# A hybrid encoder layer: where dense projections run beside the DeltaNet inverse, where the normalised operand is made, and how inverses and attention rows are finished

## The chip, the cores and the metric

The kernel runs on one core of one Trainium2 chip. The metric is device time in microseconds, the median of several runs of the whole program. One further execution was taken with the hardware profiler, and every row below is from it. The core's engines are TensorE (PE, with its weight loads as PEld), VectorE (DVE), ScalarE (ACT), GpSimd (POOL) and SyncE (SP, which here only issues DMAs). Each works through a queue of its own in order; semaphores tie them together.

## The reference, cut to what matters

There are two layers of width 1024 over 512 tokens, all float32.

```
h    = rms_norm(x, norm_mix)                    # x * rsqrt(mean(x*x)) * g
proj = h @ w_in                                 # q k v | dqkv z alpha beta | rwkv
y_att = window attention(q, k, v, sink)         # 6 heads, rotary, softmax over +-128 tokens
y_dn  = gated DeltaNet(conv(dqkv), z, ...)      # 6 heads, two directions, chunks of 64
y_rw  = RWKV-7(rwkv, ...)                       # 4 heads, two directions, chunks of 64
x = x + concat(y_att, y_dn, y_rw) @ w_out
x = x + conv_ffn(rms_norm(x, norm_ffn))
```

The DeltaNet and RWKV parts each need, for every chunk of 64 tokens, head and direction, the inverse of a unit triangular 64x64 matrix. Then a scan walks through the eight chunks. After the second layer a last rms_norm follows.

## The kernel before, in words

Activations lie transposed: 128 channels on the partitions, 512 tokens along the free axis. A float32 product is made of three fp32r products: both operands are split into a high and a low part, and `product` adds high x high, high x low and low x high in PSUM. A projection of 128 output columns has 8 blocks of 128 rows, so 24 matmuls of 512 columns (L332 to L334). The weights come by DMA in pieces of four blocks into one of three `wr` buffers; ScalarE makes the high part (L321) and GpSimd subtracts it to get the low part (L322), each with three buffers. The norm's factor `rb` (one number for each token) isn't applied before the projection: `Norm.tile_done` splits x times g, and each user of a projection multiplies its result by `rb` on VectorE while it moves it out of PSUM (`token_shift` L474, `dn_conv` L685, `rope` L867, `gate_proj` L975 and so on).

A layer goes through these steps in program order. Eight projections give RWKV's inputs. `rwkv_prep` runs for two head pairs, with DeltaNet projections and their 5-tap convolutions (`dn_conv`, four taps on VectorE, L691 and L693) between. The RWKV inverse is a chain of 30 steps of two VectorE operations on 32x32 blocks (`invert`, L403 and L404). `finish_inverse` completes the 64x64 inverses from 32x32 blocks by small matmuls (L455, L461) and copies on ScalarE (L457, L465, L469). `rwkv_scan` walks through eight steps; `dn_prep` for the three DeltaNet pairs and the five attention projections are written between them. Then `rwkv_out` runs, and the DeltaNet inverse for both directions at once (`invert_both`, L432 and L433), with an attention step after every sixth of its 31 turns. An attention step (`attn_head`) is one block of 128 queries of a pair of heads: scores (L886), masked and with a row maximum (L887), exponentials on ScalarE (L896), rows scaled by 1/sum on VectorE (L900), transposes (L903, copied by L905) and the product with v (L907). There are twelve such steps. `finish_inverse` for DeltaNet follows, then three gate projections (`gate_proj`), `dn_scan` with the remaining attention steps, `dn_out`, and the output projection: for each of eight column blocks 24 matmuls over attention, RWKV and DeltaNet rows, added to the residual (L1068). The feed-forward block ends the layer.

The queues are not simply in program order. The program is written in Tile, which at build time puts the instructions of each engine in an order: of those that are ready it takes the one that program order asks for first. An allocation waits for a free buffer of its tag. PSUM has 8 banks: two for stream `j` (dense products), three for `r`, two for `d`, one for `o`. The tag `p4` has 20 tiles of 4 KB a partition, which hold nearly everything of a layer that lives long; `t2` tiles are the short-lived 2 KB ones.

Of the kernel before, what the change touches and what calls it, by code (L numbers as in the profile page):

```python
# [14 lines left out]
P = 128  # L15
T = 512
# [20 lines left out]
def _const_array():  # L37
# [23 lines left out]
    add("m32", np.stack([hi32 - 1.0, -hi32], 1))  # L61
# [54 lines left out]
def trunk(tc, t, out):  # L116
# [21 lines left out]
    def p4(*free, dt=F32):  # L138
        return bp.tile([P, *free], dt, tag="p4", bufs=20, name=nm("p4"))
# [94 lines left out]


# [26 lines left out]
    def split(src, gcol, tag, k):  # L262
        hi = bp.tile([P, T], F32R, tag=f"hh{k}", bufs=1, name=nm("hh"))
        lo = bp.tile([P, T], F32R, tag=f"hl{k}", bufs=1, name=nm("hl"))
# [71 lines left out]
    def proj(l, parts, c0, m=P, heads=None):  # L336
# [7 lines left out]
        o = ps("j")  # L344
# [100 lines left out]
    def finish_inverse(st, o1, o2, units, upper, sign):  # L445

        ra, rb = (0, 32) if upper else (32, 0)
        n = len(units)
        for g0 in range(0, n, 16):
            grp = units[g0 : g0 + 16]  # L450
            py = ps(st)
# [7 lines left out]
            for i, (p, mt, c) in enumerate(grp):  # L459
                for h in (0, 64):  # L460
                    PE.matmul(pw[h + ra : h + ra + 32, 32 * i : 32 * i + 32], yt[h + rb : h + rb + 32, i, :], o1[h + rb : h + rb + 32, p, :], start=True, stop=True)  # L461
            for i in range(0, len(grp), 8):
                mt = grp[i][1]
# [219 lines left out]
    def dn_conv(l, o, i, rb, dst):  # L683
        u = t2("d")
        V.tensor_tensor(u, o, rb, mult)  # L685
# [466 lines left out]
```

## Time and profile before

| what | value |
|---|---|
| median of three runs | 1710.0 us (1709.49, 1710.0, 1717.93) |
| profiled execution, its own time | 1722.8 us |
| its span, first to last instruction | 1721.0 us |
| mean granted TensorE clock | 0.931 |
| TensorE busy | 1544.2 us, 90% |
| VectorE busy | 973.5 us, 57% |
| ScalarE busy | 792.0 us, 46% |
| GpSimd busy | 638.7 us, 37% |

Busy time is the time in which at least one instruction of an engine is recorded as running; matmuls overlap each other, so the mean duration of one is longer than its share of a full TensorE. [...] Times inside the profile count from the start of the span. The second layer's mixers run from about 866 to 1350 us, its feed-forward block after that.

### The profile page before, as it was taken

What the parts mean: (1) busy time and instruction counts of PE and PEld (TensorE: products, weight loads), DVE (VectorE), ACT (ScalarE), POOL (GpSimd) and SP (SyncE); (2) the same over time, 40 slices, a digit from 0 to 9 for tenths busy, and PEclk for the clock granted to TensorE, in tenths of its full rate; (3) what the DMA queues carried; (4) which work ended last, traced back from release to release, by engine and by line L of the source; (5) the groups of instructions that cost most, each with busy time, mean ns of one, the idle gap of its engine ahead of it and who ended that gap; (6) DMA issues with size and microseconds to landing.
All of it is one profiled execution on the core that took longest, in us unless ns stands there. A gap on an engine that the chain in (4) does not pass through costs nothing. (4 is left out here: it accounts for less than half of the span.)

```text
span 1721.0 us, 29049 instructions
## 1 busy us (share of the span) xinstructions
PE 1544.2 (90%) x11500; PEld 1208.7 (70%) x11500; DVE 973.5 (57%) x1595; ACT 792.0 (46%) x1493; POOL 638.7 (37%) x510
## 2 busy tenths in 40 slices
PE   7988889569999999999998887983899999999997
PEld 4676666347778888888876666652677788888885
DVE  6578946875535557731136797579563555555001
ACT  5547453355444444433336654351734544444321
POOL 4321323101265554445552112420104555555553
PEclk9989979669999999999999998995799999999998
DMA  6221211100143333333442012220003333333331
GB/s 185 73 57 38 56 38 44 37 2 20 36 122 96 98 98 95 96 104 114 119 101 68 25 45 50 55 70 1 4 19 93 102 95 97 98 99 114 101 101 65
DMA packets 230536, 126.07 MB, mean 73 GB/s; under 512 B 23656, under 2 KB 221416, under 8 KB 230400
## 3 DMA queue, kind: packets, MB, share of 16 engines
q1 hardware_dynamic: 228624, 121.02, 25.0%
q10 hardware_dynamic: 1776, 3.20, 0.6%
q8 instruction: 90, 1.47, 0.3%
q14 instruction: 46, 0.38, 0.1%
HBM read 117.84 MB, written 6.34 MB: 72 GB/s over the span
## 5 line engine op out<-in xcount | busy, mean ns | idle before, releaser
L322 POOL TENSOR_TENSOR wl<-wr,wh 128x512 fp32r<-128x512 f32 (+1 forms) x408 | 553.6, 1363 | 753.2 <-ACT wh L321 664.2
L332 PE MATMUL ps<-hh,wh 128*128 128x512 f32 x1248 | 505.2, 405 | 22.1 <-ACT wh L321 19.6
L333 PE MATMUL ps<-hl,wh 128*128 128x512 f32 x1248 | 504.5, 404 | 0.0
L334 PE MATMUL ps<-hh,wl 128*128 128x512 f32 x1248 | 500.9, 401 | 0.4 <-POOL wl L322 0.4
L321 ACT ACTIVATE wh<-wr 128x512 fp32r<-128x512 f32 (+1 forms) x408 | 246.2, 615 | 330.8 <-PE ps L333 262.4
L332 PEld LDWEIGHTS ps<-hh,wh 128*128 128x128 f32 x1248 | 237.8, 191 | 80.9 <-ACT wh L321 20.4
L333 PEld LDWEIGHTS ps<-hl,wh 128*128 128x128 f32 x1248 | 238.0, 191 | 56.8 <-issue 4.2
L334 PEld LDWEIGHTS ps<-hh,wl 128*128 128x128 f32 x1248 | 237.5, 190 | 56.8 <-issue 3.9
L1104 DVE TENSOR_TENSOR p<-ps,p 128x512 f32<-128x512 f32 x16 | 11.1, 692 | 196.6 <-PE ps L334 196.6
L332 PE MATMUL ps<-p,wh 128*128 128x512 f32 x256 | 99.6, 389 | 0.0
L333 PE MATMUL ps<-p,wh 128*128 128x512 f32 x256 | 99.6, 389 | 0.0
L334 PE MATMUL ps<-p,wl 128*128 128x512 f32 x256 | 99.6, 389 | 0.0
L903 PE MATMUL ps<-fixed,cv 128*128 128x128 f32 x120 | 24.9, 340 | 62.4 <-DVE cv L900 62.0
L1081 DVE TENSOR_TENSOR tr<-ps,rb 128x512 f32<-128x512 f32 x44 | 30.4, 691 | 80.9 <-PE ps L334 80.8
L292 POOL TENSOR_TENSOR tr<-tr,tr 128x512 f32<-128x512 f32 x32 | 42.6, 1332 | 70.4 <-ACT tr L285 59.9
L903 PEld LDWEIGHTS ps<-fixed,cv 128*128 128x128 f32 x120 | 16.0, 168 | 72.5 <-issue 44.8
L1084 DVE SCALAR_TENSOR_TENSOR td<-tr,fixed,td 128x511 f32<-128x511 f32 x44 | 42.8, 972 | 37.7 <-ACT td L1083 37.7
L285 ACT ACTIVATE tr<-p 128x512 f32<-128x512 f32 x36 | 22.6, 628 | 85.9 <-DVE p L1104 64.4
L791 POOL TENSOR_TENSOR sm<-sm,fixed 128x384 f32<-128x384 f32 x12 | 10.8, 896 | 121.5 <-DVE sm L820 64.5
L333 PEld LDWEIGHTS ps<-p,wh 128*128 128x128 f32 x256 | 48.1, 188 | 10.1
L332 PEld LDWEIGHTS ps<-p,wh 128*128 128x128 f32 x256 | 48.1, 188 | 10.1
L1084 DVE SCALAR_TENSOR_TENSOR tr<-td,fixed,tr 128x511 f32<-128x511 f32 x44 | 33.9, 771 | 37.5 <-ACT tr L1083 37.5
(294 smaller groups left out, 2559.7 us busy)
## 6 DMA issues: line engine op xcount, KB each, us to landing
wr<-ffn_w_up SPq DMA_DIRECT2D x176, 256.0 KB, 2.8
wr<-w_in SPq DMA_DIRECT2D x88, 256.0 KB, 2.9
wr<-ffn_w_down SPq DMA_DIRECT2D x80, 256.0 KB, 2.9
wr<-w_in SPq DMA_DIRECT2D x24, 128.0 KB, 2.4
p<-scr ACTq DMA_DIRECT2D x12, 256.0 KB, 3.5
wr<-w_out SPq DMA_DIRECT2D x32, 96.0 KB, 2.6
wr<-w_out SPq DMA_DIRECT2D x16, 192.0 KB, 2.9
p<-xt SPq DMA_DIRECT2D x8, 256.0 KB, 5.0
```

What stands on the lines that cost most here:

```text
L285: S.activation(sq, xk, AF.Square)
L292: G.tensor_tensor(acc, self.acc, sq, add)
L321: S.activation(hi[:, :n, :], raw[:, :n, :], AF.Copy)
L322: G.tensor_tensor(lo[:, :n, :], raw[:, :n, :], hi[:, :n, :].bitcast(F32), sub)
L332: PE.matmul(o, wh, xh, start=k == 0, stop=False)
L333: PE.matmul(o, wh, xl, start=False, stop=False)
L334: PE.matmul(o, wl, xh, start=False, stop=k == n - 1)
L791: G.tensor_tensor(gs, state, flat(gl, step), mult)
L903: PE.transpose(pp[:, P * j : P * j + P], scs[g][:, P * j : P * j + P], ident)
L1081: V.tensor_tensor(u, o, nf.rb, mult)
L1084: V.scalar_tensor_tensor(a[:, 1:], u[:, :-1], w(0), a[:, 1:], mult, add)
L1104: V.tensor_tensor(x1[j], o, x1[j], add)
```

## The change

The normalised operand is now made once. While the eight RWKV projections run, `renorm` forms x times g times `rb` and splits it under a tag of its own; every later projection of the layer uses these parts, and their users no longer multiply by `rb`. They read the product from PSUM: `dn_conv`'s taps, `token_shift` (which scales in place in PSUM), `rope`, `gate_proj`. RWKV projections rotate over four PSUM banks.

The three query projections, the three gate projections and a new piece, the RWKV rows' share of the output projection, are written as a generator `fill`, and one of its 14 parts is asked for after every second step of the DeltaNet inverse. The share of each column block is added to the residual and parked in DRAM (`xr`); the output projection then has 6 blocks instead of 8 and adds `xr`. Attention steps are no longer written into the inverse: two come before `finish_inverse`, two in each of the first three steps of `dn_scan`, then one in each.

`finish_inverse` works on 64-row halves of full width: products of 64 columns, with a shared tile `fin` that holds identity blocks beside the intermediate result, and two ScalarE copies over all 128 partitions for eight chunks, one of them with a mask as scale. `fin`'s identity blocks are written once by GpSimd. In attention the rows are scaled by ScalarE, and the sink's exponentials take the maximum as bias. The tag `p4` has 23 tiles.

```diff
-        return bp.tile([P, *free], dt, tag="p4", bufs=20, name=nm("p4"))
+        return bp.tile([P, *free], dt, tag="p4", bufs=23, name=nm("p4"))
...
+        for h in range(0, P, 32):
+            G.tensor_copy(fin[h : h + 32, 0::2, :], ident[h : h + 32, h : h + 32].unsqueeze(1).broadcast_to([32, 17, 32]))
...
-        hi = bp.tile([P, T], F32R, tag=f"hh{k}", bufs=1, name=nm("hh"))
+        hi = bp.tile([P, T], F32R, tag=f"{tag}h{k}", bufs=1, name=nm(tag + "h"))
...
             py = ps(st)
-            yt = t2(st, 16, 32)
             for i, (p, mt, c) in enumerate(grp):
                 for h in (0, 64):
-                    PE.matmul(py[h + rb : h + rb + 32, 32 * i : 32 * i + 32], mt[h + ra : h + ra + 32, c, rb : rb + 32], o2[h + ra : h + ra + 32, p, :], start=True, stop=True)
-            for h in (0, 64):
-                S.activation(yt[h + rb : h + rb + 32, : len(grp), :], py[h + rb : h + rb + 32, : 32 * len(grp)].rearrange("q (p c) -> q p c", c=32), AF.Copy)
+                    PE.matmul(py[h : h + 64, 32 * i : 32 * i + 32], mt[h + ra : h + ra + 32, c, 0:64], o2[h + ra : h + ra + 32, p, :], start=True, stop=True)
+            S.activation(fin[:, 2 * s0 + 1 : 2 * (s0 + len(grp)) : 2, :], py[:, : 32 * len(grp)].rearrange("q (p c) -> q p c", c=32), AF.Copy, scale=sign)
...
-                for h in (0, 64):
-                    S.activation(mt[h + ra : h + ra + 32, :, rb : rb + 32], pw[h + ra : h + ra + 32, 32 * i : 32 * i + 256].rearrange("q (p c) -> q p c", c=32), AF.Copy, scale=sign)
-        for i in range(0, n, 8):
-            p, mt, _ = units[i]
-            for h in range(0, P, 32):
-                S.activation(mt[h : h + 32, :, h % 64 : h % 64 + 32], o1[h : h + 32, p : p + 8, :], AF.Copy)
+                p, mt, _ = grp[i]
+                S.activation(mt[:, :, ra : ra + 32], o1[:, p : p + 8, :], AF.Copy, scale=mask)
+                S.activation(mt[:, :, rb : rb + 32], pw[:, 32 * i : 32 * i + 256].rearrange("q (p c) -> q p c", c=32), AF.Copy)
...
     def token_shift(l, o, i, rb, dst):
-        u = t2("r")
+        u = o
...
-    def dn_conv(l, o, i, rb, dst):
-        u = t2("d")
-        V.tensor_tensor(u, o, rb, mult)
+    def dn_conv(l, u, i, dst):
...
-    def rope(o, rb, scale, dst):
+    def rope(o, scale, dst):
         q = t2("r")
-        V.scalar_tensor_tensor(q, o, scale, rb, mult, mult)
+        S.activation(q, o, AF.Copy, scale=scale)
+        V.scalar_tensor_tensor(dst, o, scale, cos_t, mult, mult)
         pr = ps("r")
         PE.matmul(pr, C("rot"), q, start=True, stop=True)
-        V.tensor_tensor(dst, pr, sin_t, mult)
-        G.tensor_tensor(q, q, cos_t, mult)
+        V.tensor_tensor(q, pr, sin_t, mult)
         V.tensor_tensor(dst, dst, q, add)
...
-            V.tensor_tensor(es, sk, mxt, sub)
-            V.tensor_scalar(nmx, mxt, -1.0, None, mult)
-            S.activation(es, es, AF.Exp)
+            S.activation(nmx, mxt, AF.Copy, scale=-1.0)
...
+                S.activation(es[:, g : g + 1], sk[:, g : g + 1], AF.Exp, bias=nmx[:, g : g + 1])
...
-                V.tensor_scalar(scs[g][:, :W], scs[g][:, :W], den[:, g : g + 1], None, mult)
+                S.activation(scs[g][:, :W], scs[g][:, :W], AF.Copy, scale=den[:, g : g + 1])
...
+        def renorm(k):
+
+            xn = t2("d")
+            V.scalar_tensor_tensor(xn, x[k], norm.g[:, k : k + 1], rb, mult, mult)
+            normed.append(split(xn, None, "g", k))
...
-            o = proj(l, parts, COL_RW + P * i)
+            o = proj(l, parts, COL_RW + P * i, st="jjod"[i % 4])
...
             token_shift(l, o, i, rb, rkv[i // 2][:, i % 2, :])
+            renorm(i)
...
+        parts = normed
...
-            V.tensor_tensor(z, o, rb, mult)
-            sigmoid(sg, z)
-            V.tensor_tensor(z, z, sg, mult)
+            sigmoid(sg, o)
+            V.tensor_tensor(z, o, sg, mult)
...
+        def rwkv_share(j):
+            xo = t2("r")
+            nc.sync.dma_start(xo, xd[:, j, :])
+            o = ps("j")
+            product(o, weights(lambda raw, k0, k1: [(raw, wr[:, k0:k1, P * j : P * j + P])], 2), rw_parts)
+            V.tensor_tensor(xo, o, xo, add)
+            nc.sync.dma_start(xr[:, j, :], xo)
+
+        def fill():
+            for i in range(3):
+                qs.append(next(ap))
+                yield
+                gate_proj(i, zss[i])
+                yield
+            for j in range(KT):
+                rwkv_share(j)
+                yield
...
-            if i % 6 == 5:
-                next(att, None)
+            if i % 2 == 1:
+                next(filler, None)
         inv = run(both_ways)
+        for _ in range(2):
+            next(att)
...
         for i, _ in enumerate(dn_scan(dn)):
-            if i < 2:
-                gate_proj(1 + i, zss[1 + i])
             next(att, None)
+            if i < 3:
+                next(att, None)
...
-        mixed = [split(y, None, "h", i) for i, y in enumerate(yt + yr + yd)]
+        mixed = [split(y, None, "h", i) for i, y in enumerate(yt + yd)]
...
-            nc.sync.dma_start(xo, xd[:, j, :])
+            nc.sync.dma_start(xo, xr[:, j, :])
             o = ps("j")
-            product(o, weights(pieces, KT), mixed)
+            product(o, weights(pieces, 6), mixed)
```

## Rows read from the trace of the kernel before

**Rows 1.** Page, part 1: busy time and share of the span, instructions, by engine.

```profile
PE 1544.2 (90%) x11500; PEld 1208.7 (70%) x11500; DVE 973.5 (57%) x1595; ACT 792.0 (46%) x1493; POOL 638.7 (37%) x510
```

**Rows 2.** Windows, layer two: stretch; length; busy PE, PEld, DVE, ACT, POOL; clock; DMA.

```profile
866.00:917.00 51.00, 49.30 (x211) 37.67 (x212) 20.78 (x26) 21.20 (x35) 22.06 (x19) 1.00 0.37 93
917.00:1010.00 93.00, 77.40 (x777) 60.12 (x775) 74.95 (x99) 61.27 (x117) 17.07 (x13) 0.93 0.16 44
1010.00:1061.00 51.00, 40.28 (x296) 31.34 (x295) 49.28 (x90) 21.92 (x38) 15.88 (x12) 0.95 0.26 63
1061.00:1163.00 102.00, 89.69 (x1152) 63.59 (x1152) 61.30 (x104) 47.96 (x101) 30.54 (x35) 0.87 0.19 53
1163.00:1207.00 44.00, 19.38 (x74) 11.81 (x76) 40.21 (x105) 8.77 (x29) 0.21 (x1) 0.54 0.00 1
1207.00:1232.00 25.00, 19.38 (x422) 14.42 (x424) 11.54 (x22) 19.93 (x50) 0.00 (x0) 0.64 0.01 2
1232.00:1296.00 64.00, 60.74 (x1043) 47.63 (x1042) 38.78 (x123) 31.21 (x87) 8.31 (x8) 0.96 0.05 15
1296.00:1350.00 54.00, 49.89 (x205) 37.62 (x204) 20.04 (x26) 27.19 (x46) 31.55 (x24) 1.00 0.38 112
```

**Rows 3.** Windows, one stretch of the first feed-forward block of layer two.

```profile
1500.00:1550.00 50.00, 50.00 (x222) 41.42 (x221) 29.11 (x38) 24.23 (x37) 25.89 (x19) 1.00 0.33 95
```

**Rows 4.** Waits of 1163 to 1207: who for whom, us, times, longest.

```profile
PE ps L903 <- DVE cv L900: 30.9, 4, 15.2
```

**Rows 5.** Groups by line, 1163 to 1207: busy us, mean ns, idle before.

```profile
L433 DVE TENSOR_TENSOR pair_sq<-pair_sq,cv 128x60 f32<-128x60 f32 (+14 forms) x30 | 15.1, 503 | 0.6
...
L432 DVE TENSOR_TENSOR cv<-pair_sq 128x60 f32<-128x60 f32 (+14 forms) x30 | 15.1, 502 | 0.6
```

**Rows 6.** Groups by line, 1296 to 1350.

```profile
L1068 DVE TENSOR_TENSOR p<-ps,tr 128x512 f32<-128x512 f32 x8 | 5.4, 689 | 25.5 <-DMA tr<-xd 24.7 <-PE ps L334 0.8
```

**Rows 7.** Groups by line, 917 to 1061.

```profile
L691 DVE SCALAR_TENSOR_TENSOR cv<-td,fixed,cv 128x510 f32<-128x510 f32 (+1 forms) x16 | 14.9, 932 | 2.1 <-ACT cv L687 2.0
...
L685 DVE TENSOR_TENSOR td<-ps,rb 128x512 f32<-128x512 f32 x9 | 6.1, 681 | 0.0
```

**Rows 8.** Groups by line, 1061 to 1163.

```profile
L332 PE MATMUL ps<-hh,wh 128*128 128x512 f32 x40 | 18.8, 470 | 0.0
...
L629 POOL TENSOR_TENSOR sm<-sm,fixed 128x256 f32<-128x256 f32 x6 | 4.2, 708 | 2.4 <-DVE fixed L751 1.3 <-DVE sm L640 1.1
```

**Rows 9.** One line, 1061 to 1163 (first); timeline of ScalarE's queue (second).

```profile
L653 DVE TENSOR_TENSOR p<-ps,p x8: 408/411/425, 1084.9 to 1132.7; 128x256 f32<-128x256 f32 x8
...
1137.12 0.58 ACTq L745 DMA_DIRECT2D p<-scr  x1
```

**Rows 10.** Groups by line, 1207 to 1232.

```profile
L469 ACT ACTIVATE p<-p 32x256 f32<-32x256 f32 x23 | 9.5, 414 | 1.8 <-DVE p L440 1.5
...
L465 ACT ACTIVATE p<-ps 32x256 f32<-32x256 f32 x11 | 4.1, 375 | 1.8 <-PE ps L461 1.5
```

**Rows 11.** Timeline of VectorE, then POOL, 1022 to 1026: start, us, operation.

```profile
1024.19 1.42 DVE L404 TENSOR_TENSOR p<-p,tr 128x198 f32<-128x198 f32 x1
...
1026.19 0.36 DVE L403 TENSOR_TENSOR tr<-p 128x210 f32<-128x210 f32 x1
...
1022.27 3.12 POOL L322 TENSOR_TENSOR wl<-wr,wh 128x512 fp32r<-128x512 f32 x2 [3.77 <-ACT wh L321]
```

**Rows 12.** Groups by line, 1232 to 1296.

```profile
L332 PE MATMUL ps<-hh,wh 128*128 128x512 f32 x9 | 4.6, 510 | 0.0
...
L905 ACT ACTIVATE tr<-ps 128x384 f32<-128x384 f32 (+1 forms) x14 | 5.6, 443 | 8.6 <-PE ps L903 8.6
```

**Rows 13.** Chain that ended last, 1275 to 1280: start, us, what.

```profile
1275.34 0.89 PE ps L903 x6
...
1276.61 1.12 PE ps L907 x12
...
1278.57 0.90 PE ps L886 x4
```

More of the change, by code (lines that the diff above doesn't have):

```diff
@@ L60, in _const_array @@
     hi32 = (i % 64 >= 32).astype(np.float32)
-    add("m32", np.stack([hi32 - 1.0, -hi32], 1))
+    add("m32", np.stack([hi32 - 1.0, -hi32, 1.0 - hi32, hi32], 1))
     add("ident", np.eye(P))
@@ L233, in trunk @@
     pair_sq = cp.tile([P, 2, 32, 32], F32, name="pair_sq")
+    fin = cp.tile([P, 33, 32], F32, name="fin")
     cos_t, sin_t = fixed[:, W + DEPTH * NPAR : W + DEPTH * NPAR + T], fixed[:, W + DEPTH * NPAR + T : W + DEPTH * NPAR + 2 * T]
@@ L262, in split @@
     def split(src, gcol, tag, k):
-        hi = bp.tile([P, T], F32R, tag=f"hh{k}", bufs=1, name=nm("hh"))
-        lo = bp.tile([P, T], F32R, tag=f"hl{k}", bufs=1, name=nm("hl"))
+        hi = bp.tile([P, T], F32R, tag=f"{tag}h{k}", bufs=1, name=nm(tag + "h"))
+        lo = bp.tile([P, T], F32R, tag=f"{tag}l{k}", bufs=1, name=nm(tag + "l"))
         if gcol is None:
@@ L447, in finish_inverse @@
         ra, rb = (0, 32) if upper else (32, 0)
+        mask = C("m32")[:, 2 + ra // 32 : 3 + ra // 32]
         n = len(units)
@@ L450, in finish_inverse @@
             grp = units[g0 : g0 + 16]
+            s0 = 0
             py = ps(st)
-            yt = t2(st, 16, 32)
             for i, (p, mt, c) in enumerate(grp):
                 for h in (0, 64):
-                    PE.matmul(py[h + rb : h + rb + 32, 32 * i : 32 * i + 32], mt[h + ra : h + ra + 32, c, rb : rb + 32], o2[h + ra : h + ra + 32, p, :], start=True, stop=True)
-            for h in (0, 64):
-                S.activation(yt[h + rb : h + rb + 32, : len(grp), :], py[h + rb : h + rb + 32, : 32 * len(grp)].rearrange("q (p c) -> q p c", c=32), AF.Copy)
+                    PE.matmul(py[h : h + 64, 32 * i : 32 * i + 32], mt[h + ra : h + ra + 32, c, 0:64], o2[h + ra : h + ra + 32, p, :], start=True, stop=True)
+            S.activation(fin[:, 2 * s0 + 1 : 2 * (s0 + len(grp)) : 2, :], py[:, : 32 * len(grp)].rearrange("q (p c) -> q p c", c=32), AF.Copy, scale=sign)
             pw = ps(st)
             for i, (p, mt, c) in enumerate(grp):
+                at_i = 2 * (s0 + i) + (0 if upper else -1)
+                pair = fin.rearrange("p a b -> p (a b)")[:, 32 * at_i + 32 : 32 * at_i + 96]
                 for h in (0, 64):
-                    PE.matmul(pw[h + ra : h + ra + 32, 32 * i : 32 * i + 32], yt[h + rb : h + rb + 32, i, :], o1[h + rb : h + rb + 32, p, :], start=True, stop=True)
+                    PE.matmul(pw[h : h + 64, 32 * i : 32 * i + 32], pair[h + rb : h + rb + 32, :], o1[h + rb : h + rb + 32, p, :], start=True, stop=True)
             for i in range(0, len(grp), 8):
-                mt = grp[i][1]
-                for h in (0, 64):
-                    S.activation(mt[h + ra : h + ra + 32, :, rb : rb + 32], pw[h + ra : h + ra + 32, 32 * i : 32 * i + 256].rearrange("q (p c) -> q p c", c=32), AF.Copy, scale=sign)
-        for i in range(0, n, 8):
-            p, mt, _ = units[i]
-            for h in range(0, P, 32):
-                S.activation(mt[h : h + 32, :, h % 64 : h % 64 + 32], o1[h : h + 32, p : p + 8, :], AF.Copy)
+                p, mt, _ = grp[i]
+                S.activation(mt[:, :, ra : ra + 32], o1[:, p : p + 8, :], AF.Copy, scale=mask)
+                S.activation(mt[:, :, rb : rb + 32], pw[:, 32 * i : 32 * i + 256].rearrange("q (p c) -> q p c", c=32), AF.Copy)
     def token_shift(l, o, i, rb, dst):
-        u = t2("r")
+        u = o
         V.tensor_tensor(u, o, rb, mult)
@@ L696, in dn_conv, with dn_gates @@
         V.tensor_tensor(dst, dst, sg, mult)
-    def dn_gates(l, o, rb, scr, st):
+    def dn_gates(l, o, scr, st):
         y = t2("d")
-        V.tensor_tensor(y[:24], o[:24], rb[:24], mult)
-        V.tensor_scalar(y[:24], y[:24], C("absign")[:24], abias[l], mult, add)
+        V.tensor_scalar(y[:24], o[:24], C("absign")[:24], abias[l], mult, add)
         e, w, lw = t2("d"), t2("d"), t2("d")
@@ L909, in attn_head, with layer @@
         S.activation(dst, po, AF.Copy)
-    def layer(l, norm, xd, last):
+    def layer(l, norm, x, xd, last):
         parts, rb = norm.parts, norm.rb
+        normed = []
+        def renorm(k):
+            xn = t2("d")
+            V.scalar_tensor_tensor(xn, x[k], norm.g[:, k : k + 1], rb, mult, mult)
+            normed.append(split(xn, None, "g", k))
         rw = {"ar": [], "gb": [], "tb": [], "uv": [], "kv": []}
@@ L954, in attn_proj @@
             k = at_()
-            rope(o, rb, 1.0, k)
+            rope(o, 1.0, k)
             yield k
@@ L958, in attn_proj @@
             av = t2("r")
-            V.tensor_tensor(av, o, rb, mult)
+            S.activation(av, o, AF.Copy)
             pv = ps("r")
@@ L968, in attn_proj @@
                 q = at_()
-                rope(o, rb, 0.125, q)
+                rope(o, 0.125, q)
                 yield q
@@ L1011, in layer @@
                 qkv.append(dn_proj(2))
-            if i >= 2:
-                heads += [next(ap, None)]
-        k, vt, *qs = heads[:5]
+            if i in (2, 4):
+                heads += [next(ap)]
+        k, vt = heads
         for i in (1, 2):
@@ L1017, in layer @@
         yr = [rwkv_out(l, rw, pr_, None) for pr_ in range(2)]
-        pa, pb, pc_ = p4(2, T), p4(2, T), None
+        pa, pb, pc_ = p4(2, T), p4(2, T), p4(2, T)
         yt = [pa[:, 0, :], pa[:, 1, :], pb[:, 0, :]]
-        zss = [pb[:, 1, :]]
+        zss = [pb[:, 1, :], pc_[:, 0, :], pc_[:, 1, :]]
         att = attention()
+        qs = []
+        yh, yl = p4(2, T, dt=F32R), p4(2, T, dt=F32R)
+        for pr_, y in enumerate(yr):
+            S.activation(yh[:, pr_, :], y, AF.Copy)
+            V.tensor_tensor(yl[:, pr_, :], y, yh[:, pr_, :].bitcast(F32), sub)
+        rw_parts = [(yh[:, pr_, :], yl[:, pr_, :]) for pr_ in range(2)]
+        wo = t["w_out"][l]
+        wr = wo[768:1024].rearrange("(k p) m -> p k m", p=P)
+        xr = dp.tile([P, KT, T], F32, name=nm("xr"))
+        def rwkv_share(j):
[14 more added lines that the diff above has]
+                yield
         dpks = []
@@ L1111, in trunk @@
         norm.tile_done(k, x0[k], True)
-    xd = xk
+    xd, x = xk, x0
     for l in range(DEPTH):
-        x, norm = layer(l, norm, xd, l == DEPTH - 1)
+        x, norm = layer(l, norm, x, xd, l == DEPTH - 1)
         xd = xdram
```

20 lines of the change are left out of this document (8 added, 12 removed).

## The prediction

> **What bounds the kernel now.** I read the page's busy shares first [rows 1]: TensorE is busy 90% of the span, so a change pays only where it is not, or where it takes products off a stretch that TensorE fills. Next the stretches of the second layer [rows 2]; the first layer repeats them. I call them A (866: eight RWKV projections), B (917: RWKV preparation), C (1010: RWKV inverse), D (1061: RWKV scan, DeltaNet preparation), F (1163: DeltaNet inverse), K (1207: its completion), G (1232: DeltaNet scan), H (1296: output projection). The feed-forward stretches are not touched; there 222 matmuls fill 50 us [rows 3], so a dense product of 512 columns costs 0.225 us of TensorE where TensorE is the limit.
>
> The reader should see three things there. A, G and H are TensorE's: 49.3 of 51, 60.7 of 64, 49.9 of 54 us. B and C are VectorE's: 75.0 of 93 and 49.3 of 51. [...] The inverse itself is 15.1 + 15.1 us of VectorE [rows 5]; what is left of its 40.2, 10 us, I count to attention. In K ScalarE is busy 19.9 of 25 us and the clock is still at 0.64.
>
> **The change part by part**, one layer, against the profiled execution.
>
> *Normalised operand (A).* Eight times two VectorE operations and a ScalarE copy are added. VectorE is busy 20.8 of 51 us; 16 x 0.69 (the 512-column add [rows 6]) = 11 us more fit, and ScalarE's eight copies likewise. Cost 0, hidden by TensorE's 49.3; without that cover up to 11 us. The operand needs only x and rb, which are there from A's start, so the first later product is not late. In the first layer four POOL copies fill the new tile near the start, beside POOL's splits: I take 2 us once, between 0 and 4 (four times about one split).
>
> *Nine multiplications by rb go, taps read PSUM (B, C).* Nine of 0.681 us leave VectorE, 6.1 us [rows 7]. The taps average 0.932 us against 0.69 for an undisturbed 512-column operation, and part of that excess may go as well. VectorE is not the only limit in B and the PSUM tile is now held through four taps, where it was freed by the first operation: range 0 to -11, I take -5.
>
> *Query products leave D.* In D 3 x 40 = 120 dense products ran [rows 8], five of 24: value, three query, one gate. TensorE is busy 89.7 of 102 us. Taking out the 72 query products is worth 72 x 0.225 = 16.2 us at full clock where TensorE is the limit, 96 x 0.3 = 29 with the gate's and the slow clock (0.87 mean), 0 if the chain of the DeltaNet preparation sets the end. Two things shorten that chain as well. The big-tile pool grows from 20 to 23; in the trace the third pair's decay rows are only requested at 1137.1, just after the scan's last add at 1132.7 [rows 9], and the inverse starts 26 us after that request. And the RWKV completion loses 16 x 0.414 + 8 x 0.375 - 8 x 0.414 = 6.3 us of ScalarE, by the prices of [rows 10]. I take -15.
>
> *Fourteen pieces of dense work enter F.* Three query and three gate products and eight 6-matmul shares of the output projection are 192 x 0.225 = 43 us of TensorE, into a stretch whose inverse alone is 30 us of VectorE. VectorE gets 9 operations for the ropes, 3 for gates, 8 adds: 20 x 0.689 [rows 6] = 13.8 us. Without attention's 10 us F is 44 - 10 + 13.8 = 47.8 us. To that comes what POOL does: 12 full weight splits and 8 half ones, none of which is in F today. C shows the price: while two splits ran, an inverse operation of 198 columns took 1.42 us, and the next one, of 210 columns, 0.36 [rows 11]. That is 1.06 us for each full split, and about 0.5 for a half one (POOL's 256-column operation, 0.708 [rows 8], less what VectorE had left to do): 12 x 1.06 + 8 x 0.5 = 16.7 us if every one collides. A quarter of that is my value, since some run ahead into the three weight buffers, some meet PSUM evacuations, and some query products will still slip forward into D: 4 us, F = 52, +8. Ends: +1 (ropes outside F, 3 us of collisions) and +20 (all collide). SyncE gets eight loads and eight stores of 256 KB more; DMA's share in F is 0.00, so they are free unless a store waiting for its add holds up the next weights, which is a rival below.
>
> [...]
>
> *Completion at full width (K).* Today 23 block copies of 0.414 and 11 of 0.375 us [rows 10], 13.6 us; at full width there are two copies for eight chunks, 6 x 2 x 0.414 = 5.0, and half as many Y copies. ScalarE was busy 19.9 of 25 us, so K shortens by at most about 10; the four VectorE transposes before it and the one shared tile, which puts the groups one behind the other, stay. I take -8, between -5 and -10.
>
> *G.* It loses 3 x 9 = 27 dense products [rows 12], about 7 us with the slow ones, and gets attention: of twelve steps seven were here, two are now asked for ahead of K, so ten, three more. A step with three key blocks is 0.89 + 1.12 + 0.90 = 2.9 us of TensorE [rows 13], with 2.5 blocks on average 2.4, so +7.3. Scaling moves to ScalarE, which pays about 2 x 0.443 (the like-sized copy [rows 12]) and two small ones of at most 0.375 for each step, 1.6 x 10 = 16 us, and six operations like that copy for each of the three more steps, 8 us, against 31.2 of 64 busy: it fits. I take +2; ends -3 and +10 (if scaling on ScalarE waits behind other work).
>
> *H.* 48 of 192 products are gone, 48 x 0.225 = 10.8 us in a stretch that TensorE fills; two RWKV blocks that filled its start while the DeltaNet outputs were made are gone too, 12 x 0.225 = 2.7, of which I give back 2: -9 (-6 to -10.8).
>
> **Sum.** -5 - 15 + 8 - 8 + 2 - 9 = -27 us a layer, -54 for two, +2 for the POOL copies: -52. The profiled execution took 1722.8 us with a span of 1721.0; 1722.8 - 52 = 1670.8. The three runs have a median of 1710.0, 12.8 lower, so 1658. All low ends together are -63 a layer, all high ends +19; neither is likely, since the ends do not hang together.
>
> **Rivals.**
> 1. *POOL's splits block the inverse at full price.* F +20 instead of +8: 24 us for two layers, 1682. For: [rows 11]. Against: buffers and evacuations. 14%.
> 2. *D doesn't shrink*, because scan steps and DeltaNet preparation on VectorE and ScalarE set it: -4 (its completion only) instead of -15, 1680. For: VectorE 61.3 and ScalarE 48.0 of 102 us, in chains. Against: TensorE's 89.7. 12%.
> 3. *Nothing is held back.* The queues are ordered at build time by readiness, so query and gate products may run in D as before: D -5, F +2, G and the rest as said, -23 a layer, about 1666; only the order of products tells it from the forecast. 12%.
> 4. *Deeper:* D -25, F +2, K -10: -45 a layer, about 1622. For: D's clock. 10%.
> 5. *Attention in G waits for ScalarE*: G +20, -9 a layer, 1694. 6%.
> 6. *Slower: the inverse is queued behind evacuations in F.* VectorE works in order; each of fourteen pieces needs load, ScalarE, POOL and TensorE before its evacuation, and an evacuation placed too early stops the inverse. For: the 30.9 us of TensorE behind VectorE in just this stretch. [...] With the other terms at -35, F must grow by 35, to 79 us, that is (79 - 47.8)/14 = 2.2 us for each piece, before this decides; at 3.5 us F is 96.8, +53, 18 a layer worse: 1710 + 38 = 1748. 11%.
> The forecast itself has 35%, with a range of its own of 1640 to 1674.
>
> **How the numbers follow.** A measurement here can tell about 0.5%, that is 1701.5 and 1718.5. Faster by more: the forecast, 1 to 4 and most of 5, less some for their tails: 0.80. Within: part of 5 and tails of 1, 2 and 6: 0.08. Slower: 0.12. The range leaves out most of 6 and the lower half of 4: 1620 to 1715.
>
> **What would show it.** F about 52 us between its first and last inverse step and transposes, TensorE over 35 us busy in it at a granted clock near 1; inverse operations of 1.4 us where a split is beside them, some four to six a layer (twenty would be rival 1); K under 18 us with 12 full-width copies; D about 87; G 66; H 45, with 144 products. Long VectorE waits for TensorE inside F would be rival 6; query products ahead of F, rival 3. The forecast is wrong if D stays at 100 us or F passes 65.

## The result and the profile after

The changed kernel is slower. Its median is 1734.3 us (1729.5 to 1737.4, four runs) beside 1710.3 us for the kernel before (1709.5 to 1717.9), a ratio of 1.0125 with a 95% interval of 1.0092 to 1.0158. The forecast was 1658 with a range to 1715. The profiled execution took 1735.9 us, only 13 more than the profiled one of before, which stood at the top of that kernel's spread. So the traces account for 13 us of the 24, and kernels are compared below by the ratio of their runs on one chip.

Page, part 1, of the kernel after (as [rows 1]):

```profile
PE 1582.2 (91%) x11500; PEld 1239.9 (72%) x11500; DVE 981.1 (57%) x1519; ACT 793.8 (46%) x1539; POOL 644.7 (37%) x522
```

TensorE issues as many products as before and is busy 38 us longer. Windows of its second layer, the stretches of [rows 2] in the same order (A, B, C, D, F, K, G, H):

```profile
868.00:919.00 51.00, 49.73 (x214) 37.68 (x212) 32.94 (x42) 24.89 (x44) 23.47 (x19) 1.00 0.39 95
919.00:1005.00 86.00, 77.37 (x779) 59.16 (x777) 72.11 (x96) 61.44 (x119) 19.40 (x13) 0.96 0.18 48
1005.00:1049.00 44.00, 35.37 (x280) 27.66 (x279) 42.00 (x84) 20.76 (x36) 12.68 (x10) 0.97 0.29 72
1049.00:1139.00 90.00, 85.98 (x1110) 64.27 (x1111) 52.64 (x94) 42.48 (x88) 23.75 (x28) 0.81 0.16 43
1139.00:1203.00 64.00, 43.99 (x166) 30.24 (x164) 55.79 (x99) 17.53 (x43) 15.75 (x16) 0.79 0.35 109
1203.00:1233.00 30.00, 25.08 (x400) 22.82 (x402) 8.51 (x11) 10.02 (x27) 0.00 (x0) 0.50 0.01 2
1233.00:1303.00 70.00, 66.47 (x1060) 50.90 (x1060) 31.07 (x101) 37.70 (x111) 5.04 (x6) 0.95 0.02 6
1303.00:1361.00 58.00, 47.29 (x175) 32.62 (x176) 24.63 (x30) 28.58 (x58) 29.21 (x24) 0.90 0.33 98
```

Against [rows 2] the lengths moved by 0, -7, -7, -12, +20, +5, +6 and +4: 9 us longer where the forecast had 27 us shorter. Up to the DeltaNet inverse 26 us a layer are won; from there 35 are lost. In K the reader should see two things: ScalarE fell from 19.9 to 10.0 us as forecast, and TensorE rose from 19.4 of 25 to 25.1 of 30 at a granted clock of 0.50 (the profile gives this clock as a share of full speed).

Groups by line in K, kernel after (1203 to 1233), then the same products in the kernel before (1207 to 1232):

```profile
L468 PE MATMUL ps<-p,fin 32*64 32x32 f32 x192 | 11.1, 290 | 0.7 <-ACT fin L462 0.7
L461 PE MATMUL ps<-p,p 32*64 32x32 f32 x192 | 11.1, 290 | 5.0 <-DVE p L445 5.0
L461 PEld LDWEIGHTS ps<-p,p 32*64 32x64 f32 x192 | 10.6, 221 | 6.1 <-DVE p L445 6.1
L471 ACT ACTIVATE p<-p,fixed 128x256 f32<-128x256 f32 x6 | 3.0, 502 | 5.0 <-PE ps L461 5.0
L472 ACT ACTIVATE p<-ps 128x256 f32<-128x256 f32 x6 | 2.1, 382 | 10.5 <-PE ps L468 10.5
```

```profile
L461 PE MATMUL ps<-p,td 32*32 32x32 f32 x192 | 6.0, 216 | 1.9 <-ACT td L457 1.9
L455 PE MATMUL ps<-p,p 32*32 32x32 f32 x192 | 5.3, 221 | 3.8 <-DVE nmx L892 3.8
L461 PEld LDWEIGHTS ps<-p,td 32*32 32x32 f32 x192 | 5.0, 129 | 4.4 <-ACT td L457 3.6 <-ACT p L469 0.6 <-issue 0.2
```

The same 384 products take 22.2 us where they took 11.3 (6.0 here and 5.3 for L455), because each has 64 weight columns for 32; a weight load has a mean of 221 ns for 129. ScalarE now waits 10.5 us for TensorE. Twelve full-width copies are there as forecast and cost 5.1 us; they are no longer what ends last. TensorE waited 0.7 us for the shared tile `fin`, so that tile does not set the pace of K either. The clocks of the two stretches differ (0.50 and 0.64); the last section compares the products at one clock.

In F, groups of VectorE between first and last inverse step (1148.1 to 1203.1), and part of its timeline:

```profile
L436 DVE TENSOR_TENSOR cv<-pair_sq 128x60 f32<-128x60 f32 (+14 forms) x30 | 17.9, 595 | 0.7
L437 DVE TENSOR_TENSOR pair_sq<-pair_sq,cv 128x60 f32<-128x60 f32 (+14 forms) x30 | 16.2, 539 | 0.6
L1047 DVE TENSOR_TENSOR tr<-ps,tr 128x512 f32<-128x512 f32 x8 | 5.5, 686 | 5.3 <-PE ps L338 5.3
L887 DVE CUSTOM_DVE_ANT_0 cv<-ps,fixed 128x384 f32<-128x384 f32 (+1 forms) x6 | 3.4, 569 | 1.6 <-PE ps L886 1.6
```

```profile
1178.02 0.62 DVE L436 TENSOR_TENSOR cv<-pair_sq 128x456 f32<-128x456 f32 x1
...
1181.43 0.69 DVE L1047 TENSOR_TENSOR tr<-ps,tr 128x512 f32<-128x512 f32 x1 [2.71 <-PE ps L338]
...
1182.69 1.03 DVE L436 TENSOR_TENSOR cv<-pair_sq 128x440 f32<-128x440 f32 x1
1185.85 0.69 DVE L1047 TENSOR_TENSOR tr<-ps,tr 128x512 f32<-128x512 f32 x1 [2.12 <-PE ps L338]
```

The inverse's steps cost 34.1 us where [rows 5] add up to 30.2. At 1181.43 and 1185.85 the inverse stands still, since a share's add was put ahead of the next step and its product wasn't finished.

### The profile page after: what moved, and what is told of

The parts are those of the page before. It is cut to its first block, busy times and chain, and to the rows that moved or that the text cites. A ratio compares the mean times of both kernels' runs of the same rounds, so it can differ in the third digit from the quotient of the medians.

```text
span 1733.7 us, 28966 instructions
## 1 busy us (share of the span) xinstructions
PE 1582.2 (91%) x11500; PEld 1239.9 (72%) x11500; DVE 981.1 (57%) x1519; ACT 793.8 (46%) x1539; POOL 644.7 (37%) x522
## 3 DMA queue, kind: packets, MB, share of 16 engines
q1 hardware_dynamic: 233232, 129.41, 26.2%
## 5 line engine op out<-in xcount | busy, mean ns | idle before, releaser
L336 PE MATMUL ps<-hh,wh 128*128 128x512 f32 x928 | 367.1, 397 | 15.3 <-ACT wh L325 11.1
L337 PE MATMUL ps<-hl,wh 128*128 128x512 f32 x928 | 365.9, 394 | 6.2 <-DVE hl L274 5.8
L338 PE MATMUL ps<-hh,wl 128*128 128x512 f32 x928 | 364.3, 393 | 2.2 <-POOL wl L326 2.1
L336 PEld LDWEIGHTS ps<-hh,wh 128*128 128x128 f32 x928 | 175.3, 189 | 56.9 <-ACT wh L325 11.6
L337 PEld LDWEIGHTS ps<-hl,wh 128*128 128x128 f32 x928 | 175.5, 189 | 51.3 <-DVE hl L274 10.1
L338 PEld LDWEIGHTS ps<-hh,wl 128*128 128x128 f32 x928 | 175.3, 189 | 41.0 <-POOL wl L326 4.3
L336 PE MATMUL ps<-gh,wh 128*128 128x512 f32 (+1 forms) x288 | 121.8, 423 | 5.2 <-ACT wh L325 1.9
L338 PE MATMUL ps<-gh,wl 128*128 128x512 f32 (+1 forms) x288 | 121.7, 423 | 0.8 <-POOL wl L326 0.8
L337 PE MATMUL ps<-gl,wh 128*128 128x512 f32 (+1 forms) x288 | 120.1, 417 | 0.0
L336 PEld LDWEIGHTS ps<-p,wh 128*128 128x128 f32 x288 | 55.5, 193 | 40.9 <-issue 19.4
L338 PEld LDWEIGHTS ps<-gh,wl 128*128 128x128 f32 (+1 forms) x288 | 54.6, 190 | 16.1 <-issue 1.9
L338 PEld LDWEIGHTS ps<-p,wl 128*128 128x128 f32 x288 | 55.6, 193 | 14.4 <-POOL wl L326 1.9
```

Source lines behind the costliest of these rows:

```text
L336: PE.matmul(o, wh, xh, start=k == 0, stop=False)
L337: PE.matmul(o, wh, xl, start=False, stop=False)
L338: PE.matmul(o, wl, xh, start=False, stop=k == n - 1)
```

## The experiments

For reading them, this table gives the lengths of seven stretches of layer two, in us, each from the start or end of a named instruction in the trace. They are: the RWKV completion (last transpose of the RWKV inverse to the scan's first product); scan and preparation (to the end of the last mask add of `dn_prep`, L756 before); from there to the inverse's last step; to the last of its four transposes; the completion (to the DeltaNet scan's first product); that scan (to its last product); from there to the first add of the output projection (L1068 before). Some expectations below give the last one as 11 to 12.5 and as 16.5 us; they stop at a semaphore instruction of the add's line, 1.5 us ahead of the add in the kernel before and 3.9 us ahead in e12.

| kernel | RWKV compl. | scan, prep. | inverse | transp. | compl. | scan | to H |
|---|---|---|---|---|---|---|---|
| before | 8.0 | 83.2 | 52.9 | 8.5 | 16.1 | 63.8 | 14.0 |
| after | 18.2 | 55.9 | 78.5 | 7.8 | 22.0 | 69.8 | 18.2 |
| e1 | 8.7 | 61.5 | 71.8 | 7.6 | 14.3 | 79.1 | 17.5 |
| e2 | 18.2 | 53.4 | 63.6 | 7.6 | 21.3 | 70.4 | 16.8 |
| e3 | 18.2 | 78.1 | 54.3 | 8.5 | 28.2 | 63.7 | 14.2 |
| e4 | 8.0 | 61.9 | 74.2 | 7.4 | 14.1 | 78.3 | 14.0 |
| e5 | 8.7 | 58.8 | 66.6 | 7.6 | 15.1 | 74.3 | 16.2 |
| e6 | 8.6 | 59.3 | 66.5 | 21.3 | 19.2 | 61.6 | 14.1 |
| e7 | 19.0 | 71.5 | 54.0 | 8.4 | 26.2 | 62.2 | 14.0 |
| e8 | 7.9 | 54.5 | 68.3 | 19.1 | 19.5 | 60.0 | 14.1 |
| e10 | 7.9 | 54.5 | 68.2 | 7.6 | 14.0 | 67.2 | 18.3 |
| e11 | 8.7 | 84.2 | 54.4 | 8.4 | 18.5 | 67.6 | 14.2 |
| e12 | 18.2 | 53.6 | 75.3 | 7.4 | 20.4 | 72.2 | 15.1 |
| e13 | 8.1 | 80.1 | 54.1 | 8.5 | 14.4 | 61.0 | 13.9 |
| e14 | 7.9 | 54.5 | 69.3 | 7.5 | 13.5 | 62.1 | 17.1 |
| e15 | 7.9 | 83.8 | 54.8 | 8.4 | 19.2 | 65.4 | 14.0 |

**e1: the changed kernel with the completion of before.** `finish_inverse` is that of the kernel before, word for word; the tile `fin` and its four copies go.

> The changed kernel with the completion of the inverses as it was before (quarter-width products and copies), all else as changed. Theory A (TensorE bounds the completion at full width: its 384 products take 22 us between the inverse and the scan at a clock of 0.50, where 16 us were before, while ScalarE's saving lies idle): this stretch goes back to 16 us, 6 us a layer, 12 in all, 1722, and some more from the RWKV completion. Theory B (the whole loss of 24 us comes from the completion): 1710 or less. Theory C (the stretch is set by the transposes and copies, not by the products): no change, 1734.

1716.5 us, ratio 1.0021 (0.9994 to 1.0047), against 1.0125 with the full-width completion: some 18 us back. Theory A holds: RWKV completion 18.2 to 8.7, DeltaNet completion 22.0 to 14.3 us. Windows of the completion and the scan behind it:

```profile
1192.50:1206.80 14.30, 8.33 (x302) 7.53 (x295) 0.98 (x5) 12.99 (x32) 0.00 (x0) 0.65 0.01 3
1206.80:1286.00 79.20, 71.23 (x1078) 54.02 (x1074) 30.31 (x105) 42.59 (x125) 5.36 (x6) 0.89 0.02 5
```

ScalarE is busy 13.0 of 14.3 us, so in this kernel the old completion is ScalarE's. But the scan grew from 69.8 to 79.1 us: with 46 of attention's 60 transposes in it, where the changed kernel had 40, and a clock of 0.89, it took back what the DeltaNet completion gave. Scan and preparation, 5.6 us longer, took back more than half of the RWKV completion's 9.5 us. The other 4 us and 7 us in the inverse are what is left.

**e2: the shares back in the output projection.** `rwkv_share` and its split go; eight blocks again.

```diff
-            for j in range(KT):
-                rwkv_share(j)
-                yield
...
-        mixed = [split(y, None, "h", i) for i, y in enumerate(yt + yd)]
+        mixed = [split(y, None, "h", i) for i, y in enumerate(yt + yr + yd)]
...
-            product(o, weights(pieces, 6), mixed)
+            product(o, weights(pieces, KT), mixed)
```

> The changed kernel with the eight RWKV shares of the output projection put back into the output projection (8 blocks there); query and gate products stay held back. Theory A (the shares cost more than they give: eight adds, three stalls and two splits of VectorE, 5.5 + 5.3 + 1.7 = 12 us in the inverse, against 1 us by which the output projection shrank): inverse 12 us shorter, output projection 1 us longer, 1734 - 22 = 1712. Rival (the output projection pays the full 48 x 0.225 = 10.8 us for them): 1734 - 24 + 22 = 1732, no change.

1710.0 us, ratio 0.9957 (0.9937 to 0.9976): 24 to 29 us better than the changed kernel, as theory A had it. To the inverse's last step it takes 63.6 us for 78.5. VectorE's one wait for TensorE in the inverse is now an attention mask's (waits, 1130 to 1177.7):

```profile
DVE cv L887 <- PE ps L886: 1.7, 1, 1.7
```

From the output projection's first add to its last it took 38.2 us for 34.8: the 48 products taken out of it bought 3 us there, not 10.8.

**e3: nothing held back.** Queries in the RWKV scan, gates behind the completion, attention after every sixth turn, eight blocks; the rest as changed.

```diff
-            if i in (2, 4):
-                heads += [next(ap)]
-        k, vt = heads
+            if i >= 2:
+                heads += [next(ap, None)]
+        k, vt, *qs = heads[:5]
...
-            if i % 2 == 1:
-                next(filler, None)
+            if i % 6 == 5:
+                next(att, None)
```

> The changed kernel with nothing held back: query products in the RWKV scan, gate products after the completion, attention steps in the inverse and eight blocks in the output projection, as before; normalised operand, PSUM reads, 23 big tiles, full-width completion and ScalarE's row scaling as changed. Theory A (the holding back costs more than it gives, the rest gains 12 us a layer up to the end of the RWKV inverse and loses 6 in the completion): 1710 - 12 = 1698, inverse 40 us. Rival (all that was gained ahead of the DeltaNet inverse came from the query products that left; the rest only loses 6 in the completion): 1722.

1738.3 us, ratio 1.0134 (1.0110 to 1.0158). Both expectations failed: it is slower than the rival's 1722 too. The inverse is back (54.3 us), but scan and preparation take 78.1, and the completion, with six dense products of a gate in it, 28.2. So holding back was not simply the loss.

**e4: holding back alone,** in the kernel before: its `layer` with `fill`, `rwkv_share`, six blocks, attention moved and 23 big tiles.

> The kernel before with the holding back alone (fourteen pieces in the inverse, attention moved behind it, 23 big tiles so that there is room); products still multiplied by rb, old completion, rows scaled by VectorE. Theory A (the holding back is what loses: inverse +20, scan and preparation -15, later stretches +4 a layer): 1710 + 18 = 1728. Rival (holding back gains, the other parts spoil it): 1690 or less.

1744.4 us, ratio 1.0164 (1.0140 to 1.0189); the rival is out, the loss larger than theory A had. In layer two the inverse takes 74.2 us, scan and preparation 61.9, the DeltaNet scan 78.3 (63.8 before).

**e5: e1 and e2 together.**

> The changed kernel with the old completion and with the RWKV shares back in the output projection. Theory A (two separate losses, one in the completions, one in the inverse): they add up, 1734 - 18 - 24 = 1692. Rival (each freed the same slack, so that the second finds none): 1710.

1703.6 us, ratio 0.9931 (0.9902 to 0.9960), between the two expectations: the losses are separate, but they don't add up in full. What is left over is the DeltaNet scan, 74.3 us.

**e6: e5 with attention in the inverse as before.**

```diff
             if i % 2 == 1:
                 next(filler, None)
+            if i % 6 == 5:
+                next(att, None)
         inv = run(both_ways)
-        for _ in range(2):
-            next(att)
```

Also one step for each scan step.

> As the run with both undone, and attention steps again asked for after every sixth turn of the inverse and one for each scan step, as before; query and gate products stay held back. Theory A (attention moved out of the inverse makes the scan the place where TensorE queues for it: completion and scan 92 to 94 us in every kernel with that move, 80 before): inverse 5 us longer, completion and scan 93 to 76 us, net 12 a layer, 1692 - 24 = 1668. Rival (the work of attention is the same wherever it stands, and VectorE's part of it in the inverse costs what the scan gains): 1692.

1702.7 us, ratio 0.9929 (0.9903 to 0.9955): the rival. The scan gave 13 us back (74.3 to 61.6), but the last of the four transposes behind the inverse came after 21.3 us for 7.6; e8's timeline shows why.

**e7: the full-width completion alone,** in the kernel before.

> The kernel before with the full-width completion alone. Theory A (TensorE bounds it: RWKV completion 8 to 18 us, DeltaNet 16 to 22 or 28, some of it refilled by the dense products that wait meanwhile): 10 to 16 us a layer slower, 1730 to 1745. Prediction's own term (ScalarE bounds it, half the copies): 8 us a layer faster, 1699.

1737.6 us, ratio 1.0135 (1.0107 to 1.0163). This edit by itself costs 23 us by the ratio; theory A holds, and the prediction's own term had the wrong sign. RWKV completion 19.0 for 8.0, DeltaNet completion 26.2 for 16.1. Scan and preparation are 11.7 us shorter behind the first of them (71.5 for 83.2), so in layer two it is the DeltaNet completion whose 10 us are lost.

**e8: e6 with masked copies and narrow products.**

```diff
-        for i in range(0, n, 8):
-            p, mt, _ = units[i]
-            for h in range(0, P, 32):
-                S.activation(mt[h : h + 32, :, h % 64 : h % 64 + 32], o1[h : h + 32, p : p + 8, :], AF.Copy)
...
+                p, mt, _ = grp[i]
+                for r in (ra, rb):
+                    S.activation(mt[:, :, r : r + 32], o1[:, p : p + 8, :], AF.Copy, scale=C("m32")[:, 2 + r // 32 : 3 + r // 32])
```

They stand ahead of the copies of the product, which stay.

> As the run with attention in the inverse, with a completion that keeps the quarter-width products and replaces the four 32-partition copies of the diagonal blocks for eight chunks by two masked ones over 128 partitions. Theory A (the products were what cost, ScalarE bounds the old completion with 13 of 14.3 us): 2 x 0.41 - (2 x 0.50 - 2 x 0.41) = 0.66 us less for each of 10 groups of eight chunks, some 3 us in the DeltaNet completion and 2 in the other, 1668 - 8 = 1660. Rival (the completion waits for its products or transposes, not for ScalarE): no change against that run.

1688.5 us, ratio 0.9849 (0.9819 to 0.9879), 14 us better than e6 where theory A had 8. But theory A's place was wrong: the completions hardly moved (7.9 for 8.6 and 19.5 for 19.2), and the largest part, 4.8 us a layer, is in scan and preparation, where 44 dense products ran for 54. Its VectorE timeline behind the inverse's last step shows the wait of e6 too:

```profile
1166.53 0.22 DVE L434 TENSOR_TENSOR pair_sq<-pair_sq,cv 128x60 f32<-128x60 f32 x1
1171.62 0.48 DVE L883 CUSTOM_DVE_ANT_0 cv<-ps,fixed 128x256 f32<-128x256 f32 x1 [4.86 <-PE ps L882]
...
1174.34 0.16 DVE L892 TENSOR_TENSOR den<-den,es 128x2 f32<-128x2 f32 x1 [1.82 <-ACT es L891]
...
1174.62 1.93 DVE L441 STREAM_TRANSPOSE p<-pair_sq 128x1024 f32<-128x1024 f32 x1
1179.24 0.48 DVE L883 CUSTOM_DVE_ANT_0 cv<-ps,fixed 128x256 f32<-128x256 f32 x1 [2.69 <-PE ps L882]
```

The inverse ended at 1166.5 and its transposes were ready, yet the first starts at 1174.6: masks of the two last attention steps stand ahead of it in VectorE's queue, each waiting for scores.

**e10: e8 with three attention steps in the inverse,** one behind the completion.

```diff
-            if i % 6 == 5:
-                next(att, None)
+            if i in (5, 11, 17):
+                next(att)
...
         dn["o"] = [p4(2, T), p4(2, T)]
+        next(att)
```

> The run with masked copies and attention in the inverse (1688.5), with three attention steps there in place of five, one more behind the completion and one for each scan step. Theory A (the last two steps of the five run behind the inverse's last step, and their masks stand in VectorE's queue ahead of the four transposes that the completion waits for: 19 us to the last transpose, 8 without them): 11 us less there a layer, two steps more in the scan at 2.9 to 6 us each, net 1 to 5 us a layer, 1678 to 1686. Rival (a step costs the scan what it cost there): 1688.

1679.3 us, ratio 0.9788 (0.9739 to 0.9837): theory A. Windows of inverse, transposes and completion:

```profile
1103.90:1156.50 52.60, 32.62 (x127) 21.44 (x126) 47.71 (x95) 19.76 (x48) 12.03 (x9) 0.77 0.17 45
1156.50:1164.10 7.60, 7.60 (x88) 5.81 (x88) 7.47 (x5) 4.25 (x9) 0.00 (x0) 0.50 0.00 0
1164.10:1178.00 13.90, 9.93 (x320) 9.05 (x320) 1.12 (x6) 11.76 (x32) 0.00 (x0) 0.50 0.02 4
```

Transposes 7.6 us for 19.1, completion 13.9 for 19.5; the scan grew by 7.

**e11: the normalised operand, PSUM reads, 23 tiles and ScalarE's rows alone** (e3 with the completion of before).

> The changed kernel with nothing held back and the old completion: what is left of the change is the normalised operand, the PSUM reads, 23 big tiles and the rows scaled by ScalarE. Theory A (these gain 12 us a layer by the end of the RWKV inverse, as in every run so far, and lose some of it in the RWKV scan, where 81 dense products ran in 59 us and 78 in 62 before): 5 to 10 us a layer, 1696 to 1706. Rival (the difference of 1 us between the run with nothing held back and the full-width completion alone is their worth: none): 1716.

1712.8 us, ratio 0.9982 (0.9957 to 1.0007): nearer the rival. The RWKV inverse ends 14 us earlier in its layer, but 131 dense products remain for scan and preparation where 116 ran before, and completion and DeltaNet scan are 6 us longer (18.5 and 67.6).

**e12: attention rows scaled by VectorE,** all else as changed.

```diff
-                S.activation(scs[g][:, :W], scs[g][:, :W], AF.Copy, scale=den[:, g : g + 1])
+                V.tensor_scalar(scs[g][:, :W], scs[g][:, :W], den[:, g : g + 1], None, mult)
```

> The changed kernel with the attention rows scaled by VectorE again. Theory A (ScalarE is busy 37.7 of 70 us in the scan and has room; the scaling lies beside other work): 1734 within 4. Rival (attention in the scan waits for ScalarE, whose scaling takes 0.60 us a row block where VectorE took 0.38): 5 to 10 us a layer faster, 1714 to 1724.

1720.1 us, ratio 1.0020 (0.9992 to 1.0048): 14 to 18 us faster, so theory A falls. The windows from the scan's last product to the first add of the output projection, here and in the changed kernel:

```profile
1292.30:1307.40 15.10, 10.52 (x28) 5.51 (x28) 9.29 (x13) 8.50 (x16) 3.62 (x3) 0.91 0.11 33
1302.70:1320.90 18.20, 12.99 (x41) 7.68 (x42) 8.88 (x15) 12.10 (x27) 3.09 (x3) 0.81 0.08 23
```

That is 3 us of a layer's gain. In the changed kernel ScalarE still scales and copies attention's last rows there, between its steps for the DeltaNet outputs (L362):

```profile
1304.54 0.91 ACT L899 ACTIVATE cv<-cv,den 128x256 f32<-128x256 f32 x2
1305.86 0.69 ACT L362 ACTIVATE td<-ps,fixed 128x512 f32<-128x512 f32 x1 [0.41 <-PE ps L856]
...
1308.30 0.60 ACT L908 ACTIVATE p<-ps 128x512 f32<-128x512 f32 x1 [0.69 <-PE ps L906]
```

**e13: masked copies alone,** in the kernel before.

> The kernel before with one edit: the four 32-partition copies of the diagonal blocks for eight chunks become two masked ones over 128 partitions; products stay at a quarter of the width. Theory A (ScalarE bounds the old completion): 0.66 us less for each of 10 groups of eight chunks, up to 6 us a layer, 1704 to 1710. Rival (the completion waits for products, or TensorE has other work there): 1716.

1710.6 us, ratio 0.9973 (0.9947 to 0.9999): within theory A, at the edge of what can be told, and a third of what the same copies gave in e8. The DeltaNet completion is 1.7 us shorter, the RWKV completion is not.

**e14: e10 with rows scaled by VectorE.**

> The best version so far (1679.3: masked completion, no shares, three attention steps in the inverse) with attention rows scaled by VectorE. Theory A (ScalarE's scaling delays attention, which ends 7 us after the scan and holds up the DeltaNet outputs: 16.5 us from the scan's end to the output projection, 11 to 12.5 wherever attention ends first): 4 to 7 us a layer, 1665 to 1671. Rival (it cost only where two attention steps stood in one scan step): 1679.

1675.4 us, ratio 0.9765 (0.9710 to 0.9819), the best version. It is 4 us under e10 by the medians; the intervals overlap, so it doesn't decide between the two. In the profile the scan is 5 us shorter, but attention still ends behind it and the way to the output projection is 17.1 us, 1.2 less than in e10: the place I named is not where it gained.

**e15: e14's parts with nothing held back** (attention after every sixth turn as before).

> The changed kernel with masked quarter-width completion, rows scaled by VectorE, eight blocks in the output projection, and nothing held back: query products in the RWKV scan, gate products after the completion, attention in the inverse as before. Theory A (holding back queries and gates is itself worth 10 us a layer and more: without it scan and preparation take 84 us from the RWKV completion on where the best version takes 54): 1712.8 less 5 for the masks and 0 to 8 for the rows, 1700 to 1708. Rival (the best version's gain is that of the mended parts): 1680.

1709.5 us, ratio 0.9959 (0.9934 to 0.9984): theory A. With the other parts mended, holding back queries and gates (with attention's places) is worth the step from 0.9959 to 0.9765, some 33 us: scan and preparation take 54.5 us for 83.8, the inverse 69.3 for 54.8.

## Why the prediction was wrong, by its own steps

Two steps of the sum failed most: the completion, whose products had no price (K), and the shares of the output projection, whose cost was set too low (F) and whose worth too high (H).

**Operand and taps (0 and -5).** A stayed at 51 us with VectorE at 32.9, as worked out. B and C gave 14 us, near the sum of what VectorE lost: 6.1 of multiplications, 1.8 in the RWKV inverse, and 5.3 of taps, which now read PSUM. One of their two groups (905 to 1049), 932 ns in [rows 7]:

```profile
L692 DVE SCALAR_TENSOR_TENSOR cv<-ps,fixed,cv 128x510 f32<-128x510 f32 (+1 forms) x16 | 11.8, 742 | 1.6 <-ACT cv L688 1.5
```

In the kernel before three of this group's 16 taps took 1.67 to 1.78 us, each beside a weight split of GpSimd, and the others at most 0.75 us. In the changed kernel none took more than 0.75 us, though the one at 1014.54 ran beside a split (1014.41 to 1015.78). Why a tap that reads PSUM was not longer beside a split was not shown. I had these terms and took less than half of their sum. But e11 shows that much of the gain is given back by the end of the layer.

**D (-15).** It came to -12, with a term of the wrong sign inside: the RWKV completion, for which I had taken off 6.3 us, grew by 10 (8.0 to 18.2). Part of that came back behind it: e1, without the wide completion, takes 70.2 us for completion, scan and preparation together where the changed kernel takes 74.1, so the wrong sign cost D some 4 us. The queries did stay back: 34 dense products ran in scan and preparation, 116 before. Rivals 2 and 3 are out.

**Completion (-8 in K): the first step that failed.** I read ScalarE's 19.9 of 25 us, priced its copies, and gave the products no price, though their weight columns double. TensorE set the new pace: K grew by 5 us and the RWKV completion by 10. e1, e7 and e13 show it from three sides: 18 us back without it, 23 lost with it alone, and no loss but 5 us gained when the copies widen and the products stay narrow. e8's 14 us don't belong here, since its completions are as long as e6's.

**F (+8).** It was +20. Two terms held: evacuations (3 ropes, 3 gates and 8 adds; forecast 13.8, by the groups 12.3) and POOL's collisions with the inverse's steps, 4 us forecast and 34.1 - 30.2 = 3.9 measured; rival 1, the full price, is out, although F came to its +20. But that 4 met 3.9 is partly luck: only 3 full and 9 half splits ran beside the inverse's steps, 7.7 us at the full price, so half of it was paid and not a quarter, and in e1 the same steps took 37.9 us. TensorE was busy 44.0 us in F, but at a clock of 0.79 where I had said near 1. Three things I left out. Attention did not leave the inverse: steps written behind it were ready and ran inside, 5 us of VectorE. Waits for evacuations and masks were 6.9 us where before had 2.5. And the inverse's first step came 9.5 us behind the last extraction of the first direction's diagonal blocks, where it had come 4.9 us behind it. Timelines of VectorE, with GpSimd's splits beside it, after first, then before:

```profile
1138.46 1.75 DVE L1036 TENSOR_TENSOR p<-p,p 128x512 fp32r<-128x512 f32 x1
1140.13 3.36 DVE L424 SCALAR_TENSOR_TENSOR p<-p,fixed 128x256 f32<-128x256 f32 x3
...
1140.09 1.29 POOL L326 TENSOR_TENSOR wl<-wr,wh 128x512 fp32r<-128x512 f32 x1 [0.43 <-ACT wh L325]
1141.64 1.57 POOL L326 TENSOR_TENSOR wl<-wr,wh 128x512 fp32r<-128x512 f32 x1 [0.26 <-ACT wh L325]
```

```profile
1162.21 1.28 DVE L420 SCALAR_TENSOR_TENSOR p<-p,fixed 128x256 f32<-128x256 f32 x3
```

A split of the RWKV rows for the shares (L1036) now stands there, and the second direction's three extractions took 1.1 us each, where 0.43 had done: weight splits run beside them now, as in [rows 11], so POOL's part of F is some 2 us more than I counted, before the inverse's first step. Rival 6 named the right queue, but its waits for share adds are 5.3 us, far from the 2.2 us for each piece at which it would decide alone; e2 takes these waits away and the shares' adds with them.

**G (+2).** +6. I had charged attention's TensorE time and found ScalarE room. Kernels with 36 of a layer's 60 attention transposes in the scan took 60 to 68 us there, those with 43 to 50 took 70 to 79, those with 40 took 62 to 70. ScalarE's scaling, rival 5 at 6%, has a price, 14 to 18 us for two layers by e12, though before that run I argued that it would be nothing. But it is not paid in the scan, as rival 5 had it: e12's scan is not shorter; its gain lies ahead of the scan and behind it.

**H (-9): the other step that failed, with F.** +4 in that stretch. Two parts of the sum were wrong. Attention ends 5.6 us behind the scan's last product, where it used to end 3 us before, so the DeltaNet outputs wait: in the kernels where it ends first the output projection's first add comes 13.9 to 15.1 us behind the scan, in the others 16.2 to 18.3. And from the scan's end to that add 23 dense products ran where 36 did. TensorE time taken from a stretch is gained only while TensorE stays full: here it is busy 47.3 of 58 us, where [rows 2] have 49.9 of 54.

Sum by layer: -14 for B and C, -12, +20, +5, +6, +4 = +9 in the second; the first layer's last step stands 2.7 us later, which with 9 and the end gives the 13 us of the profiled pair. Against the forecast's -27 a layer that is 36 us: K and H missed by 13 each, F by 12, G by 4 and D by 3, and B and C gave 9 more than I took.

## What to carry to other kernels

Before work is taken off one engine, price the same edit on every engine it touches: the wide copies halved ScalarE's time and doubled that of 384 small products. Dense work put into a VectorE chain pays (33 us here, with attention's places) if its evacuations are few and come from products that are done in time; eight small shares with an add each cost more than the products they moved. In an in-order queue, look at what stands ahead of the instruction on which the next stage waits: two attention masks ahead of four transposes made 8 us of them 19.

## What the runs showed of the hardware that I had not expected

Windows of the RWKV completion and its first 128 products, before and after:

```profile
1062.80:1070.80 8.00, 5.53 (x195) 5.20 (x196) 1.17 (x2) 5.61 (x13) 0.00 (x0) 0.50 0.02 5
L455 PE MATMUL ps<-p,p 32*32 32x32 f32 x128 | 4.1, 237 | 8.3 <-DVE p L411 8.3
1050.60:1068.80 18.20, 18.16 (x267) 16.18 (x267) 4.53 (x5) 5.90 (x14) 1.27 (x1) 0.50 0.19 45
L461 PE MATMUL ps<-p,p 32*64 32x32 f32 x128 | 7.2, 290 | 7.2 <-DVE p L415 7.2
```

At a clock of 0.50 in both kernels, a product with 32 rows and 32 moving columns took 0.032 us with 32 weight columns and 0.056 us with 64 (128 in 4.1 and in 7.2 us). Whether the weight load or the product itself sets this pace was not separated. Through the 22.1 us of the wide DeltaNet completion TensorE was busy 21.4 us and its granted clock stayed at 0.50. And the time of the kernel before went with its mean granted clock: of 19 executions on one chip, the quickest took 1709.1 us at 0.938 and the slowest 1722.5 at 0.928.
